# The first stage of a two-layer diffusion trunk: TensorE and SyncE in the source's own order, modulation rows as one stream

## Chip, core and metric

The kernel runs on one core of one Trainium2 chip. The metric is the device time of one execution in microseconds (us). Four compute engines matter: TensorE (PE in the profile, with PEld for its weight loads), VectorE (DVE), ScalarE (ACT), and SyncE (SP), whose queue issues nearly all loads from HBM.

## What is computed

A trunk of two layers over 256 latent tokens of width 2048, with 256 context tokens for the first layer. Cut to what matters here:

```python
s_lat, s_ctx = silu(c), silu(c_ctx)
for l in range(2):
    m = s_lat @ ada_w[l] + ada_b[l]                    # 2048 x 12288, six rows of modulation
    sh1, sc1, g1, sh2, sc2, g2 = split(m, 6)
    h = rms(xs, norm1_g[l]) * (1 + sc1) + sh1
    if l == 0:
        mc = s_ctx @ ada_w[l] + ada_b[l]
        hc = rms(ctx, norm1_g[l]) * (1 + csc1) + csh1
        y = attention(h, hc)                           # q, k, v by one input projection
    else:
        y = hyena(h)                                   # long convolution with filters from a small net
    xs = xs + g1 * y
    xs = xs + g2 * conv_ffn(rms(xs, norm2_g[l]) * (1 + sc2) + sh2)
```

The filters of the second layer (`_hyena_filters`: a net of three layers with sines, a projection to 2 x 2 x 2048 channels, a decay, a spectrum) depend on parameters alone. They, like the modulation rows, can be computed at any time before their use.

## The kernel before

Matrix products take the weights in chunks of 256 rows by 512 columns (`wload`, L321 to L324, 512 KB, from SyncE's queue). `wsplit` parts a chunk into a high and a low half (ACT cast L329, DVE subtraction L330), and `products` (L333 to L339) adds three products of halves. The tiles of `raw` have six buffers, `whi` and `wlo` three each, `araw` six. PSUM has eight banks; a `Ring` hands them out in turn.

The **first stage** ends when the first of the five key and value projections (`kv0`) is multiplied. Three pieces of work run in it beside each other:

- *Modulation rows for the first norm.* Scale (`j = 1`) and shift (`j = 0`) of 2048 columns each, latent and context together, in four groups `g` of 512 columns. `ada_block(g)` loads eight chunks for each `j`, two at a time, and multiplies them (L917: four matmuls of 32 rows by 512 columns for a pair of chunks, all into one bank `pv`). A block of eight chunks ends with a copy `st` by ACT (L921), a selection on PE (L924) into a bank `pt`, and DVE additions that write `adaV` and `cada` (L926) and the gains (L929). There are eight blocks, called ada10, ada00, ada11 and so on, each of four steps.
- *The filters.* `filter_net` (three layers, L539 to L549, each a matmul, a chain of DVE operations and a sine) and then `filters`: for each of four column groups and two orders a pair of filters. Each of the two has two `samples` (three matmuls L342 to L344 into a bank, DVE product with the decay L584, ACT cast L353, DVE rest L354, ACT absolute value L586, DVE maximum L589 from the second on). After the second of a pair `pn` sums the magnitudes on PE (L596 on DVE, then L599), and its reciprocal is taken by DVE (L571). `spectra` of a filter (two banks, six matmuls, one ACT copy L610, two DVE combinations L613, two stores) follow the samples of the next one. These generators are stepped by `bg`, with a credit of `START_RATE` per step of the modulation rows.
- *The norms* of the latent and the context rows. `stream_norm` loads the rows (L644), squares them (ACT L655, DVE additions L659), sums them over channels on PE and takes the inverse root on DVE (`rstd_of`, L371 to L387: L377 on PE, `newton`, L385 on DVE, L386 on PE), and multiplies (L664). `Normed.get` (L397 on) applies gain and shift and parts the result into halves (L415 to L420).

From the second group on, two chunks of `kv0` (`in_proj`, L744 on, 24 matmuls each) are put in per group; the last two follow behind the groups.

The instructions are traced in the order of the source, but the order on each engine's queue is set by a scheduler. It goes through all traced instructions with its own estimate of the times and picks the ready ones by priority. Each engine then works its queue strictly in that order. `tc.high_priority` raises the priority of a block of instructions: the weight matmuls of `ada_block` are in one.

The remaining ten modulation rows are computed from transposed weights by DVE, as weighted sums: `Ada.one` (L467 to L487) loads 512 KB on SyncE and, four steps later, multiplies and adds up a tile with one DVE instruction (L481). `drive` (L311) runs a stage and steps these sums at a rate per stage; `need` forces what is still missing when a row must be complete. `HY_ADA` is the rate of the second layer's input projection and `HO_ADA` that of its output projection. A list cell `calm[0]` puts the rate to zero while true; `proj_out` sets it anew for each of its groups (true in the last), and `ffn` for each of its eighths (true in the first two of the first chunk). The input projection of the second layer does not set it.

Of the kernel before, what the change touches and what calls it, by code (L numbers as in the profile page):

```python
# [21 lines left out]
T = 256  # L22
# [157 lines left out]
PI_F = 3.1415925  # L180


START_RATE = 2.0, 1.4
Q_RATE = 6.5
O_RATE = 5.2
KV_ADA, Q_ADA, O_ADA, HY_ADA, HO_ADA = 1.9, 0.7, 0.8, 0.2, 0.2
F0_ADA, F1_ADA = (0.7, 0.6), (0.4, 0.2)
EV_RATE, FLY, LAG = 1.0, 8, 4
F_RATE, HY_RATE, HO_RATE = 0.3, 1.2, 2.0
# [3 lines left out]
def trunk_kernel(ctx, tc, out, xT, cT, cols, rows, f_w0, f_w12, f_w3, ada_w, ada_t, w_in, w_out, hw_in, hw_out,  # L193
                 wg, wv, wd, k_tab, k_fg, k_z, k_decay):
    nc = tc.nc
# [172 lines left out]
        V.tensor_scalar(t, t, 0.375, 1.875, op0=ALU.mult, op1=ALU.add)  # L368
        V.tensor_tensor(y, y, t, op=ALU.mult)

    def rstd_of(accs, ps):  # L371

        pss = ps()
        n = len(accs)
        for tt in range(2):
            for i, a in enumerate(accs):
                PE.matmul(pss[:, tt: tt + 1], a[:, tt * P:(tt + 1) * P], ones[:, 0:1], start=i == 0, stop=i == n - 1)  # L377
        v = tiny([P, 2])
        V.tensor_scalar(v, pss[:, 0:2], 1.0 / D, EPS, op0=ALU.mult, op1=ALU.add)
        y = tiny([P, 2])  # L380
        newton(y, v, 2)
        pb = ps()
        dg = s2([P, T])
        for tt in range(2):
            V.tensor_scalar(dg[:, tt * P:(tt + 1) * P], ident, y[:, tt: tt + 1], None, op0=ALU.mult)  # L385
            PE.matmul(pb[:, tt * P:(tt + 1) * P], ones, dg[:, tt * P:(tt + 1) * P], start=True, stop=True)  # L386
        return pb[:, 0:T]  # L387

    def square_into(acc, x, first):
        if first:  # L390
# [249 lines left out]
    def load_x(src, name):  # L640
        g = []
        for i in range(4):
            t = q4([P, 4, T], F32, name)
            SP.dma_start(t, src[:, 4 * i:4 * i + 4])  # L644
            g.append(t)
        return g

    def stream_norm(src, res):
        xg = load_x(src, "x0")
        res.extend(xg)  # L650
        yield
        acc = None
        for g in range(4):
            sq = q4([P, 4, T], F32, "sq0")
            A.activation(sq, xg[g], AF.Square)  # L655
            if acc is None:
                acc = sq
            else:
                V.tensor_tensor(acc, acc, sq, op=ALU.add)  # L659
            yield  # L660
        pb = rstd_of([acc[:, k] for k in range(4)], ST)
        for g in range(4):
            for k in range(4):
                V.tensor_tensor(xg[g][:, k], xg[g][:, k], pb, op=ALU.mult)  # L664
            yield
# [236 lines left out]
    ftag[0] = Ring(6, 7, 2, 3)  # L902
    g0, gc0 = (pool.tile([P, KT], F32, tag="gain", bufs=2, name=nm("g")) for _ in range(2))

    def ada_block(g):

        gs = slice(4 * g, 4 * g + 4)

        tags = ("raw", "whi", "raw", "wlo"), ("raw", "araw", "raw", "araw")
        for j in (1, 0):  # L910
            lab[0] = f"ada{j}{g}"
            pv = AD()
            for i in range(0, 8, 2):
                raws = [wload(ada_w[i + n, 4 * j + g], tags[g > 0][(i + n) % 4]) for n in range(2)]
                with tc.high_priority():
                    for q in range(4):
                        PE.matmul(pv[32 * q:32 * q + 32], sl[:, 2 * i + q], raws[q // 2][:, q % 2],  # L917
                                  start=i == 0, stop=i == 6, tile_position=(0, 32 * q))
                yield
            st = s2([P, 512], F32, "adast")  # L920
            A.copy(st, pv)  # L921
            pt = AD()
            for b in range(4):
                PE.matmul(pt[:, 2 * b:2 * b + 2], st[:, b * P:(b + 1) * P], sel, start=True, stop=True)  # L924
            for s, dst in enumerate((adaV[:, 0, j, gs], cada[:, j, gs])):
                V.tensor_tensor(dst, pt[:, 0:8].rearrange("p (b s) -> p b s", s=2)[:, :, s], col("ada_b", j * KT + 4 * g, 4), op=ALU.add)  # L926
            if j == 1:
                for a, sc in ((g0, adaV[:, 0, 1, gs]), (gc0, cada[:, 1, gs])):
                    V.scalar_tensor_tensor(out=a[:, gs], in0=sc, scalar=1.0, in1=col("n1", 4 * g, 4), op0=ALU.add, op1=ALU.mult)  # L929

    bg.add(filter_net(), "filters")
    bg.add(filters(range(4)), "filters")
    norm_bg = Bg()
    xg, cg = [], []
    norm_bg.add(stream_norm(xT, xg), "nx")
    norm_bg.add(stream_norm(cT, cg), "nc")
    hN = Normed(xg, None, g0, adaV[:, 0, 0])
    cN = Normed(cg, None, gc0, cada[:, 0])
    KV0 = QC
    kvs = (("kv", KV0 + 2048, 0), ("k", KV0, 0), ("k", KV0 + 512, 1), ("v", KV0 + 1024, 0), ("v", KV0 + 1536, 1))  # L940
    for _ in range(3):
        bg.one()
    norm_bg.one()
    for _ in range(3):
        bg.one()
    first = None
    for g in range(4):
        for i, _ in enumerate(ada_block(g)):
            bg.step(START_RATE[g > 0])
            norm_bg.step(5.0)  # L950
            if g and i in (4, 7):
                lab[0] = "kv0"
                next(first)
        if not g:
            norm_bg.drain()
            ftag[0] = Ring(6, 7)
            banks = LO4.four()
            first = in_proj(kvs[0][1], banks, True)
        hN.get(g)
        cN.get(g)  # L960
    lab[0] = "kv0"
    for _ in range(3):
        bg.step(1.0)
    for _ in first:
        bg.step(4.0)
    bg.drain()
    spread_s(HI4)
    ada_bg.add(*ADA_LATER)
    attn_tables()
# [146 lines left out]
    accs = []  # L1116
# [195 lines left out]
```

## Time and profile before

| | |
|---|---|
| median of 3 runs | 2642.45 us (2640.13 to 2645.43) |
| profiled execution | 2640.06 us, span 2638.3 us |
| mean granted clock of TensorE | 0.976 |
| PE busy | 2525.4 us, 96% of the span |
| DVE busy | 1968.6 us, 75% |
| ACT busy | 1259.7 us, 48% |
| first stage, 0 to 246.2 us | PE busy 180.4 us |

A row of a timeline gives start, us, engine, source line, operation, the tile written and the tiles read (buffer numbers left out), shapes and count; in brackets the idle time of the engine just before it and what ended that. In a row of a group of instructions, the figures after the bar are busy us and the mean ns of one, then idle time before them with its releasers. A waits row gives the total, the number of waits and the longest. The granted clock is 1.00 at full speed.

### The profile page before, as it was taken

How to read it: one execution, taken by the hardware profiler on the slowest of the kernel's cores; microseconds unless marked ns; L12 is line 12 of the kernel's file. 1: busy time of each engine (PE TensorE's matmuls, PEld its weight loads, DVE VectorE, ACT ScalarE, POOL GpSimd, SP SyncE). 2: the span in 40 equal slices, each digit the busy share in tenths (PEclk: the TensorE clock that was granted, in tenths of full speed). 3: DMA queues.
4: the chain of work that ended last, by engine and by line, in shares of the span. 5: the costliest groups of instructions: out<-in, count | busy, mean ns of one | idle time of the engine just before them, and what ended most of it. 6: DMA issues, size and time to landing. Idle time of an engine off the chain costs nothing.

```text
span 2638.3 us, 48119 instructions
## 1 busy us (share of the span) xinstructions
PE 2525.4 (96%) x19502; PEld 2349.1 (89%) x19502; DVE 1968.6 (75%) x3073; ACT 1259.7 (48%) x1803; POOL 0.7 (0%) x6
## 2 busy tenths in 40 slices
PE   4788999999899999999999999999799999999999
PEld 2456888668899999999999999998799999999999
DVE  5656876987788888888886778889776755556664
ACT  3345223665354444445553656554354444445543
POOL 0000000000000000000000000000000000000000
PEclk7888999999999999999999999999899999999999
DMA  8685877655779999998898565555778766666664
GB/s 291 209 300 203 271 266 260 197 165 160 255 262 327 328 333 326 327 329 316 307 323 290 189 199 176 178 167 201 247 246 268 259 193 193 193 195 193 196 207 138
DMA packets 178870, 638.67 MB, mean 242 GB/s; under 512 B 20087, under 2 KB 20184, under 8 KB 178648
## 3 DMA queue, kind: packets, MB, share of 16 engines
q1 hardware_dynamic: 174040, 627.22, 71.5%
q10 hardware_dynamic: 4608, 8.39, 0.8%
q8 instruction: 152, 2.49, 0.4%
q14 instruction: 70, 0.57, 0.1%
HBM read 622.94 MB, written 12.58 MB: 241 GB/s over the span
## 4 chain that ended last, share of the span: by engine, by line
PE 89%; DVE 5%; ACT 3%; DMA 2%; issue 1%; SPq 0%; ACTq 0%; DVEq 0%
PE ps_proj L338 23%; PE ps_hy L338 9%; PE ps_kv L338 7%; PE ps_q L338 3%; PE ps_attn L846 1%; PE ps_ada L917 1%; PE ps_attn L807 1%; PE ps_ada L338 1%; DMA w<-f_w 1%; DVE araw_ada L481 1%; PE ps_conv L342 1%; DMA raw_kv<-w_in 1%; PE ps_filters L342 1%; PE ps_conv L343 1%; PE ps_conv L344 0%
## 5 line engine op out<-in xcount | busy, mean ns | idle before, releaser
L330 DVE TENSOR_TENSOR wlo_proj<-raw_proj,whi_proj 128x1024 fp32r<-128x1024 f32 x240 | 292.4, 1222 | 149.0 <-ACT whi_proj L329 147.1
L329 ACT CAST whi_proj<-raw_proj 128x1024 fp32r<-128x1024 f32 x240 | 252.0, 1054 | 306.9 <-PE ps_proj L338 271.6
L481 DVE SCALAR_TENSOR_TENSOR araw_ada<-araw_ada,slB 128x1024 f32<-128x1024 f32 x320 | 387.6, 1217 | 0.0
L338 PE MATMUL ps_proj<-ph,whi_proj 128*128 128x256 f32 x1408 | 192.4, 277 | 0.1
L338 PE MATMUL ps_proj<-ph,wlo_proj 128*128 128x256 f32 x1408 | 191.6, 276 | 0.0
L338 PE MATMUL ps_proj<-pl,whi_proj 128*128 128x256 f32 x1408 | 191.2, 276 | 0.0
L338 PEld LDWEIGHTS ps_proj<-ph,whi_proj 128*128 128x128 f32 x1408 | 174.3, 188 | 0.9 <-ACT whi_proj L329 0.9
L338 PEld LDWEIGHTS ps_proj<-ph,wlo_proj 128*128 128x128 f32 x1408 | 174.1, 188 | 0.2 <-DVE wlo_proj L330 0.2
L338 PEld LDWEIGHTS ps_proj<-pl,whi_proj 128*128 128x128 f32 x1408 | 174.1, 188 | 0.0
L329 ACT CAST whi_hy<-raw_hy 128x1024 fp32r<-128x1024 f32 x96 | 101.3, 1056 | 105.0 <-PE ps_hy L338 76.3
L330 DVE TENSOR_TENSOR wlo_hy<-raw_hy,whi_hy 128x1024 fp32r<-128x1024 f32 x96 | 116.3, 1221 | 44.2 <-ACT whi_hy L329 44.2
L338 PE MATMUL ps_hy<-hhi,whi_hy 128*128 128x256 f32 x768 | 109.1, 282 | 1.1 <-ACT hhi L418 1.1
L338 PE MATMUL ps_hy<-hlo,whi_hy 128*128 128x256 f32 x768 | 106.5, 280 | 0.0
L338 PE MATMUL ps_hy<-hhi,wlo_hy 128*128 128x256 f32 x768 | 104.3, 278 | 0.0
L338 PEld LDWEIGHTS ps_hy<-hhi,whi_hy 128*128 128x128 f32 x768 | 99.4, 190 | 3.4 <-ACT hhi L418 1.4
L338 PEld LDWEIGHTS ps_hy<-hlo,whi_hy 128*128 128x128 f32 x768 | 97.6, 190 | 0.8
L338 PEld LDWEIGHTS ps_hy<-hhi,wlo_hy 128*128 128x128 f32 x768 | 95.7, 188 | 0.1
L329 ACT CAST whi_kv<-raw_kv 128x1024 fp32r<-128x1024 f32 x40 | 42.0, 1053 | 110.7 <-PE ps_kv L338 82.5
L330 DVE TENSOR_TENSOR wlo_kv<-raw_kv,whi_kv 128x1024 fp32r<-128x1024 f32 x40 | 48.9, 1223 | 38.7 <-ACT whi_kv L329 38.7
L338 PE MATMUL ps_kv<-whi_kv,hhi 128*128 128x512 f32 x256 | 66.5, 400 | 0.0
L338 PE MATMUL ps_kv<-wlo_kv,hhi 128*128 128x512 f32 x256 | 64.0, 391 | 0.0
L338 PE MATMUL ps_kv<-whi_kv,hlo 128*128 128x512 f32 x256 | 63.9, 392 | 0.0
(9814 smaller groups left out, 7616.3 us busy)
## 6 DMA issues: line engine op xcount, KB each, us to landing
araw_ada<-ada_t SPq DMA_DIRECT2D x320, 512.0 KB, 5.1
raw_proj<-wd SPq DMA_DIRECT2D x176, 512.0 KB, 4.4
raw_hy<-hw_in SPq DMA_DIRECT2D x96, 512.0 KB, 3.8
raw_ada<-ada_w SPq DMA_DIRECT2D x46, 512.0 KB, 8.2
raw_kv<-w_in SPq DMA_DIRECT2D x40, 512.0 KB, 4.9
raw_q<-w_in SPq DMA_DIRECT2D x32, 512.0 KB, 4.6
raw_proj<-w_out SPq DMA_DIRECT2D x32, 512.0 KB, 4.5
raw_proj<-hw_out SPq DMA_DIRECT2D x32, 512.0 KB, 4.5
```

The costliest lines, as they stand in the source:

```text
L329: A.copy(hi, raw)
L330: V.tensor_tensor(lo, raw, hi, op=ALU.subtract)
L338: PE.matmul(o, ll if p == 2 else lh, rl if p == 1 else rh, start=first and p == 0, stop=last and p == 2, skip_group_check=True)
L342: PE.matmul(o, lh, rh, start=first, stop=False, **kw)
L343: PE.matmul(o, lh, rl, start=False, stop=False, **kw)
L481: V.scalar_tensor_tensor(out=raw, in0=raw, scalar=1.0, in1=slB[:, h * 1024:(h + 1) * 1024], op0=ALU.mult, op1=ALU.mult, accum_out=acc[:, h ...
L807: PE.matmul(ss_[m], qT[64 * m:64 * m + 64, h % 4, q_], KTa[h // 2][64 * m:64 * m + 64, h % 2], start=True, stop=True)
L846: PE.matmul(o[:, 0:P], wT[:, kt * P:(kt + 1) * P], v, start=kt == 0, stop=kt == 3)
L917: PE.matmul(pv[32 * q:32 * q + 32], sl[:, 2 * i + q], raws[q // 2][:, q % 2], start=i == 0, stop=i == 6, tile_position=(0, 32 * q))
```

## The change

Inside the first stage, TensorE and SyncE no longer take their order from the scheduler: `tc.manual_schedule` keeps their instructions in the order of the source. The other engines are still scheduled. The modulation rows become one generator, `ada_stream`. Where a block ended with copy, selection and additions at once, `columns` now does the copy at the block's end and the selection one step later, behind the first weight matmuls of the next block; its bank comes from the filters' ring instead of the blocks' own. Both norms' rows are loaded before the stream starts. The inverse root (`rstd_steps`) becomes two steps, with three steps of the norm's queue between. The rates change: 1.5 filter steps per step of the rows in the first group and 1.8 in the others (2.0 and 1.4 before), 3 norm steps instead of 5, and two steps of the filters ahead of the stream instead of six. `HY_ADA` goes from 0.2 to 0.3 and `HO_ADA` from 0.2 to 0.4.

```diff
-START_RATE = 2.0, 1.4
+START_RATE = 1.5, 1.8
...
-KV_ADA, Q_ADA, O_ADA, HY_ADA, HO_ADA = 1.9, 0.7, 0.8, 0.2, 0.2
+KV_ADA, Q_ADA, O_ADA, HY_ADA, HO_ADA = 1.9, 0.7, 0.8, 0.3, 0.4
...
-    def rstd_of(accs, ps):
+    def rstd_steps(accs, ps):
...
         newton(y, v, 2)
+        yield
         pb = ps()
...
-        return pb[:, 0:T]
+        yield pb[:, 0:T]
...
-    def stream_norm(src, res):
-        xg = load_x(src, "x0")
-        res.extend(xg)
-        yield
+    def stream_norm(xg):
...
-        pb = rstd_of([acc[:, k] for k in range(4)], ST)
+        rest = rstd_steps([acc[:, k] for k in range(4)], ST)
+        next(rest)
+        for _ in range(3):
+            yield
+        pb = next(rest)
...
+    def ada_stream():
+        def columns(g, j, pv):
+            gs = slice(4 * g, 4 * g + 4)
             st = s2([P, 512], F32, "adast")
             A.copy(st, pv)
-            pt = AD()
+            yield
+            pt = ftag[0]()
...
+            else:
+                hN.get(g)
+                cN.get(g)
+            yield
+
+        before = None
+        for g in range(4):
+            tags = ("raw", "araw", "raw", "araw") if g else ("raw", "whi", "raw", "wlo")
+            for j in (1, 0):
+                pv = AD()
+                for i in range(0, 8, 2):
+                    raws = [wload(ada_w[i + n, 4 * j + g], tags[(i + n) % 4]) for n in range(2)]
+                    for q in range(4):
+                        PE.matmul(pv[32 * q:32 * q + 32], sl[:, 2 * i + q], raws[q // 2][:, q % 2],
+                                  start=i == 0, stop=i == 6, tile_position=(0, 32 * q))
+                    if before:
+                        next(before)
+                        before = None
+                    yield g, 4 * (j == 0) + i // 2
+                before = columns(g, j, pv)
+                next(before)
+        next(before)
...
-    for _ in range(3):
-        bg.one()
-    norm_bg.one()
-    for _ in range(3):
-        bg.one()
-    first = None
-    for g in range(4):
-        for i, _ in enumerate(ada_block(g)):
+    with tc.manual_schedule(engines={nc.tensor.engine, nc.sync.engine}):
+        for _ in range(2):
+            bg.one()
+        xg.extend(load_x(xT, "x0"))
+        cg.extend(load_x(cT, "x0"))
+        norm_bg.add(stream_norm(xg), "nx")
+        norm_bg.add(stream_norm(cg), "nc")
+        first = None
+        for g, i in ada_stream():
             bg.step(START_RATE[g > 0])
-            norm_bg.step(5.0)
+            norm_bg.step(3.0)
             if g and i in (4, 7):
                 lab[0] = "kv0"
                 next(first)
```

Line numbers move with the edits: L599 of before is L603 after, L917 is L942, L924 is L921, L386 is L387, L481 is L485.

How the rows stand on SyncE's queue near the program's start, first before the change. `raw_ada` are chunks of weights for the modulation rows, `x` the latent (`xT`) or context (`cT`) rows:

```order
L323 DMA raw_ada_153_564<-ada_w 128x1024
L323 DMA raw_ada_174_640<-ada_w 128x1024
L644 DMA x_308<-cT 128x1024
L644 DMA x_310<-cT 128x1024
L644 DMA x_312<-cT 128x1024
L644 DMA x_314<-cT 128x1024
L323 DMA raw_ada_175_642<-ada_w 128x1024
```

The same place after it:

```order
L648 DMA x_144<-xT 128x1024
L648 DMA x_146<-cT 128x1024
L648 DMA x_148<-cT 128x1024
L648 DMA x_150<-cT 128x1024
L648 DMA x_152<-cT 128x1024
L323 DMA raw_ada_46_155<-ada_w 128x1024
L323 DMA raw_ada_47_157<-ada_w 128x1024
```

The four loads of context rows stood behind fourteen loads of weights; now they stand ahead of the first.

On PE, in the first group, before (`ps_nc` is the context rows' norm, `ps_ada` a block of the modulation rows):

```order
L377 MATMUL ps_nc_375<-ones_67,sq_364 128x1 x8
L386 MATMUL ps_nc_398<-s_399,ones_67 128x128 x2
L342 MATMUL ps_filters_485<-w_349,fah_176 128x512
L343 MATMUL ps_filters_485<-w_349,fah_176 128x512
L344 MATMUL ps_filters_485<-w_349,fal_177 128x512
L917 MATMUL ps_ada_124_464<-raw_ada_125_465,sl 32x512 x2
L917 MATMUL ps_ada_124_464<-raw_ada_126_467,sl 32x512 x2
L917 MATMUL ps_ada_124_464<-raw_ada_133_495,sl 32x512 x2
L917 MATMUL ps_ada_124_464<-raw_ada_134_497,sl 32x512 x2
L917 MATMUL ps_ada_124_464<-raw_ada_144_533,sl 32x512 x2
```

And after it, the second block of the rows, between its second and its third pair of chunks:

```order
L942 MATMUL ps_ada_88_314<-raw_ada_100_354,sl 32x512 x2
L342 MATMUL ps_filters_360<-w_259,fah_211 128x512
L343 MATMUL ps_filters_360<-w_259,fah_211 128x512
L344 MATMUL ps_filters_360<-w_259,fal_212 128x512
L603 MATMUL ps_filters_371<-ones_67,hf_290 128x1 x4
L342 MATMUL ps_filters_376<-fhl_284,fm_249 128x512
L343 MATMUL ps_filters_376<-fhl_285,fm_249 128x512
L344 MATMUL ps_filters_376<-fhl_284,fm_249 128x512
L342 MATMUL ps_filters_377<-fhl_284,fm_249 128x512
L343 MATMUL ps_filters_377<-fhl_285,fm_249 128x512
L344 MATMUL ps_filters_377<-fhl_284,fm_249 128x512
L377 MATMUL ps_nc_395<-ones_67,sq_344 128x1 x8
```

A block's sixteen matmuls stood together, behind the context norm; now pairs of chunks stand between filter matmuls, and `pn` (L603) stands right behind the sample matmuls from which its magnitudes come.

On DVE, ahead of the last mixer, before (`t` are the steps of the inverse root, `araw_ada` the weighted sums of modulation rows):

```order
L379 TENSOR_SCALAR t_20631<-ps_proj_3349_20620 128x2
L481 SCALAR_TENSOR_TENSOR araw_ada_20113,asum_14253<-araw_ada_20113,slB_86 128x1024
L359 TENSOR_SCALAR t_20634<-t_20631 128x2
L481 SCALAR_TENSOR_TENSOR araw_ada_20274,asum_14253<-araw_ada_20274,slB_86 128x1024
L360 TENSOR_SCALAR t_20633<-t_20634 128x2
L481 SCALAR_TENSOR_TENSOR araw_ada_20583,asum_14253<-araw_ada_20583,slB_86 128x1024
L362 TENSOR_TENSOR t_20634<-t_20633 128x2
L481 SCALAR_TENSOR_TENSOR araw_ada_20586,asum_14253<-araw_ada_20586,slB_86 128x1024
L363 SCALAR_TENSOR_TENSOR t_20634<-t_20634,t_20631 128x2
L481 SCALAR_TENSOR_TENSOR araw_ada_20589,asum_14253<-araw_ada_20589,slB_86 128x1024
```

And after it:

```order
L379 TENSOR_SCALAR t_20634<-ps_proj_3349_20623 128x2
L485 SCALAR_TENSOR_TENSOR araw_ada_20338,asum_14256<-araw_ada_20338,slB_86 128x1024
L359 TENSOR_SCALAR t_20637<-t_20634 128x2
L485 SCALAR_TENSOR_TENSOR araw_ada_20417,asum_14256<-araw_ada_20417,slB_86 128x1024
L360 TENSOR_SCALAR t_20636<-t_20637 128x2
L485 SCALAR_TENSOR_TENSOR araw_ada_20604,asum_14256<-araw_ada_20604,slB_86 128x1024
L362 TENSOR_TENSOR t_20637<-t_20636 128x2
L330 TENSOR_TENSOR wlo_ffn1.0_3367_20710<-raw_ffn1.0_3365_20707,whi_ffn1.0_3366_20709 128x1024
L363 SCALAR_TENSOR_TENSOR t_20637<-t_20637,t_20634 128x2
```

Before, nine weighted sums stand between the steps of the inverse root there; after, three, and six more stand earlier, in the output projection of the second layer.

More of the change, by code (lines that the diff above doesn't have):

```diff
@@ L386, in rstd_of @@
             PE.matmul(pb[:, tt * P:(tt + 1) * P], ones, dg[:, tt * P:(tt + 1) * P], start=True, stop=True)
-        return pb[:, 0:T]
+        yield pb[:, 0:T]
+    def rstd_of(accs, ps):
+        return list(rstd_steps(accs, ps))[1]
     def square_into(acc, x, first):
@@ L903, in trunk_kernel @@
     g0, gc0 = (pool.tile([P, KT], F32, tag="gain", bufs=2, name=nm("g")) for _ in range(2))
[L905 to L919, printed above, removed]
+    def ada_stream():
+        def columns(g, j, pv):
+            gs = slice(4 * g, 4 * g + 4)
             st = s2([P, 512], F32, "adast")
             A.copy(st, pv)
-            pt = AD()
+            yield
+            pt = ftag[0]()
             for b in range(4):
@@ L929, in ada_block @@
                     V.scalar_tensor_tensor(out=a[:, gs], in0=sc, scalar=1.0, in1=col("n1", 4 * g, 4), op0=ALU.add, op1=ALU.mult)
+            else:
[8 more added lines that the diff above has]
+                for i in range(0, 8, 2):
+                    lab[0] = f"ada{j}{g}"
+                    raws = [wload(ada_w[i + n, 4 * j + g], tags[(i + n) % 4]) for n in range(2)]
[9 more added lines that the diff above has]
+        next(before)
     bg.add(filter_net(), "filters")
@@ L934, in trunk_kernel @@
     xg, cg = [], []
-    norm_bg.add(stream_norm(xT, xg), "nx")
-    norm_bg.add(stream_norm(cT, cg), "nc")
     hN = Normed(xg, None, g0, adaV[:, 0, 0])
@@ L953, in trunk_kernel @@
                 next(first)
[L954 to L966, printed above, removed]
+            if (g, i) == (0, 7):
+                norm_bg.drain()
+                ftag[0] = Ring(6, 7)
+                banks = LO4.four()
+                first = in_proj(kvs[0][1], banks, True)
+        lab[0] = "kv0"
+        for _ in first:
+            bg.step(4.0)
+        bg.drain()
     spread_s(HI4)
```

## The prediction

> **What bounds the kernel now.** I read the busy time by stage first. Columns: stretch, length, busy us (and instructions) of PE, PE's weight loads, DVE, ACT, POOL, then PE's granted clock, the DMA share and GB/s.
>
> ```profile
> 0.00:77.70 77.70, 42.12 (x154) 22.39 (x154) 46.53 (x121) 22.92 (x35) 0.70 (x6) 0.74 0.71 257
> 77.70:206.50 128.80, 105.55 (x536) 64.36 (x532) 79.00 (x153) 62.27 (x114) 0.00 (x0) 0.89 0.77 269
> 206.50:246.20 39.70, 32.71 (x133) 25.30 (x130) 23.86 (x60) 19.62 (x43) 0.00 (x0) 0.83 0.61 217
> 246.20:300.00 53.80, 53.80 (x232) 42.39 (x231) 38.54 (x74) 19.55 (x36) 0.00 (x0) 1.00 0.68 227
> ```
>
> From 246.2 us on PE has no idle time, so whatever the first stage gains or loses there is passed on one to one. In the first 246.2 us PE is busy for 180.4, at a clock below full. No other engine is full either: DVE 149.4, ACT 104.8, DMA share about 0.7. So the stage is set by the order in which work stands on each queue. PE's timeline shows where (start, us, operation, idle before it and who ended it); the cuts of the table above are the ends of the second and the eighth block of modulation rows (L917) and of kv0's last product.
>
> ```profile
> 9.00 1.11 PE L539 MATMUL ps_filters<-s,s 64*64 64x256 f32 x2 [3.39 <-ACT s L549]
> 12.82 3.14 PE L917 MATMUL ps_ada<-raw_ada,sl 128*32 128x512 f32 x8 [2.71 <-DVE s L546]
> 29.62 1.05 PE L917 MATMUL ps_ada<-raw_ada,sl 128*32 128x512 f32 x4
> 52.02 1.86 PE L599 MATMUL ps_filters<-ones,hf 128*128 128x1 f32 x8 [5.16 <-DVE hf L596]
> 54.32 0.63 PE L343 MATMUL ps_filters<-fhl,fm 128*128 128x512 f32 x1
> 54.75 0.63 PE L344 MATMUL ps_filters<-fhl,fm 128*128 128x512 f32 x1
> 58.21 0.39 PE L343 MATMUL ps_filters<-w,fah 128*128 128x512 f32 x1
> 58.44 0.40 PE L344 MATMUL ps_filters<-w,fal 128*128 128x512 f32 x1
> 64.86 3.57 PE L377 MATMUL ps_nc<-ones,sq 128*128 128x1 f32 x16 [6.03 <-DVE sq L659]
> 73.42 4.37 PE L917 MATMUL ps_ada<-raw_ada,sl 128*32 128x512 f32 x32
> 97.02 3.64 PE L917 MATMUL ps_ada<-raw_ada,sl 128*32 128x512 f32 x32 [3.16 <-ACT adast L921]
> 203.79 2.76 PE L917 MATMUL ps_ada<-raw_kv,sl 128*32 128x512 f32 x24
> 244.41 2.00 PE L338 MATMUL ps_ada<-whi_kv,hlo 128*128 128x512 f32 x8
> ```
>
> Between 30.7 and 73.4 us no row of weights is multiplied; then a whole block comes in one lump of 4.4 us. A matmul of 512 columns starts every 0.43 us at 54 us (half clock) and every 0.23 us at 58 us. SyncE's queue, and its longest wait in the first 250 us, show the same hole from the side of the loads:
>
> ```profile
> 28.03 4.17 SPq L644 DMA_DIRECT2D x<-cT  x4
> 41.08 5.22 SPq L323 DMA_DIRECT2D raw_ada<-ada_w  x4
> 55.06 0.33 SPq L323 DMA_DIRECT2D raw_kv<-ada_w  x1
> SPq L323 <- PE ps_ada L917: 58.5, 19, 17.4
> ```
>
> The context rows `cT` are asked for behind fourteen weight loads; PE's matmuls of its norm stand ahead of the second block and wait 6.03 us for its squares; the block holds the buffers; SyncE waits 17.4 us at a stretch for one.
>
> **The change, part by part.** *Start.* Four loads of 512 KB (`cT`) now precede the first weights. The rate by 6.25 us slices:
>
> ```profile
> GB/s 176 402 406 337 409 409 400 341 115 75 0 42 252 334 86 110 329 344 271 141 273 365 245 370 327 213 144 345 351 212 343 348 194 326 369 369 81 79 161 95
> ```
>
> At about 405 GB/s each takes 1.3 us, so the first weight matmul goes from 12.8 to about 18.0 us, a loss of 5.2 at most, since PE waits there for a filter layer too. It buys the end of the hole: all later weights find free buffers as long as PE consumes them two by two.
>
> *First two blocks.* Before, they end at 77.7 us with 42.1 busy. After: 18.0, plus 39.9 of work (42.1 less 2.2 for two layers of the filter net, done by then), less 6.5 for 15 filter matmuls that the new order has later (21 against 36, at 0.43), plus waits. The waits on PE's side, before:
>
> ```profile
> PE ps_filters L342 <- ACT w L353: 11.2, 4, 4.8
> PE ps_filters L599 <- DVE hf L596: 10.7, 3, 5.2
> PE ps_ada L917 <- ACT adast L921: 5.7, 2, 3.2
> PE ps_nx L386 <- DVE s L385: 2.6, 1, 2.6
> ```
>
> I keep 3.5 for L599, 2.6 for the first norm's second half (the second's is covered by the weight and filter matmuls put between) and 4, an estimate between 0 and 7, for the filter net's layers, which now stand behind weight matmuls. 18.0 + 33.4 + 10 = 61.4, say 62.
>
> *The six blocks that follow.* Work: 105.6 x 0.89 = 94 us at full clock. The new order has 159 filter matmuls here against 123 and 120 of kv0 against 128: 28 more at 0.23 is 6.4, and one more L599 and L924 group about 2. So 102, and at the same clock 102 / 0.89 = 115. Waits: what goes are the late loads of filter weights (11.2 us in four waits; they are now asked for many blocks ahead) and the block's bank (`adast`, 5.7), as its copy and its selection are now two steps apart. What comes is the price of source order: `pn` (L603, before L599) stands right behind the sample matmuls that feed it, in six of eight places without a kv0 product between. Its chain, from the groups of the first 251 us:
>
> ```profile
> L584 DVE TENSOR_TENSOR hf<-ps_filters,dec 128x512 f32<-128x512 f32 x32 | 21.4, 686 | 15.4 <-PE ps_filters L344 15.4
> L613 DVE SCALAR_TENSOR_TENSOR spo<-ps_filters,se 128x512 f32<-128x512 f32 x32 | 21.0, 685 | 10.7 <-PE ps_filters L344 6.3 <-issue 1.5 <-ACT hhi L416 1.2
> L589 DVE TENSOR_TENSOR hf<-hf,hf 128x512 f32<-128x512 f32 x16 | 10.8, 689 | 1.3 <-ACT hf L586 1.0
> L596 DVE TENSOR_TENSOR hf<-hf,hf 128x512 f32<-128x512 f32 x8 | 5.5, 689 | 0.2
> L353 ACT CAST fhl<-hf 128x512 fp32r<-128x512 f32 x32 | 19.4, 619 | 46.0 <-DVE hf L584 45.6 <-DVE hlo L420 0.3
> L586 ACT ACTIVATE hf<-hf 128x512 f32<-128x512 f32 x32 | 19.4, 625 | 4.5 <-DVE fhl L354 4.3
> ```
>
> 0.69 + 0.62 + 0.63 + 0.69 + 0.69 is 3.3 us, with its hand-overs 3.5. Four of the six fall in this stretch: 14 us. Two banks serve samples, spectra, `pn` and now also the modulation's selection; a bank read by two L613 (1.3 us) holds the sample behind it, about 1 us for each of six pairs: 6. Sum 20, against 23 before (128.8 less 105.6). The bounds are 6, if weight and kv0 matmuls cover most of them, and 53, if none (below). 115 + 20 = 135.
>
> *The end of the stage.* 32.7 x 0.83 = 27 at full clock, less 13 matmuls (3.0) and about 1 of the sums that spread the conditioning row, which come later: 23, or 26 at 0.89; one L603 wait with what is left of the last norm's tail is 4. So 30, and kv0 ends at 62 + 135 + 30 = 227 instead of 246.2: 19 gained. The added steps of the norms and of the stream add no instruction of weight (cost 0; the same matmuls and squares are issued), and from kv1 to the middle of the second layer all engines keep their order.
>
> *Late rates.* `HY_ADA` is read only where `calm[0]` is false; the first mixer leaves it true and the next `proj_out` is the first to clear it, so 0.2 to 0.3 moves nothing. `HO_ADA` counts: 28 of 32 steps advance it, 5 units before (28 x 0.2), 11 after, and the forced rest ahead of the last mixer falls from 11 to 5. There DVE is what PE waits for (first and last weighted sum of the nine between the norm's steps, then PE's next matmul, and a stretch of the convolutions before it):
>
> ```profile
> 1893.98 0.16 DVE L379 TENSOR_SCALAR t<-ps_proj 128x2 f32<-128x2 f32 x1 [1.81 <-PE ps_proj L377]
> 1894.06 1.22 DVE L481 SCALAR_TENSOR_TENSOR araw_ada<-araw_ada,slB 128x1024 f32<-128x1024 f32 x1
> 1895.27 1.22 DVE L481 SCALAR_TENSOR_TENSOR araw_ada<-araw_ada,slB 128x1024 f32<-128x1024 f32 x1
> ...
> 1903.79 1.22 DVE L481 SCALAR_TENSOR_TENSOR araw_ada<-araw_ada,slB 128x1024 f32<-128x1024 f32 x1
> 1907.43 0.48 DVE L385 TENSOR_SCALAR s<-ident,t 128x128 f32<-128x128 f32 x2
> 1907.77 1.22 PE L386 MATMUL ps_proj<-s,ones 128*128 128x128 f32 x4 [13.82 <-DVE s L385]
> 1780.00:1840.00 60.00, 57.70 (x424) 52.29 (x424) 56.91 (x101) 27.35 (x40) 0.00 (x0) 1.00 0.57 198
> ```
>
> Nine sums become three: 6 x 1.215 = 7.3 us, less 0.7 for small steps that they hid. Three of the six land in the convolutions' end, where DVE has 3.1 us free in 60 and needs 3.6: a cost between 0 and 3.7, I take 2.6. Net 4.0.
>
> **Sum.** 19 + 4 = 23. The profiled execution took 2640.06 us (span 2638.3 and 1.8 around it), 2.4 under the median of the runs; from the median, 2642.45 - 23 = 2619.
>
> **The rivals.** *Waits covered* (chance 0.17): weight and kv0 matmuls cover the filters' chain and keep the clock up. For: six of the largest waits above are of things that came late, not of work. Against: PE's order is fixed, so a cover works only where it stands. Six blocks in 102 + 6, end in 26, start in 60: kv0 ends at 194, 52 gained, with the late part 56: 2586.
>
> *The clock* (0.18): PE slows after short waits. After the wait of 5.16 us the matmuls run at half speed for six us. At a granted 0.80 instead of 0.89 the six blocks take 102 / 0.80 + 20 = 148: 13 less gained, 2632. The Trainium skill, "TensorE: Matmul & The Clock Gate", Part 1 (the HAM clock gate), has PE fall to half rate once it idles for a window of about 3.4 us and come back after about as long of steady work. By that rule the 3.5 us at L603 would trip it each time; the trace agrees at 52 us.
>
> *Slower: two banks in line* (0.12). PE can no longer step over a filter matmul whose bank is not free. A pair of filters (its samples, spectra and one `pn`) is then one chain: two L613 1.3 us, sample 0.7, L584 0.7, half a spectrum 0.7, two L613 1.3, sample 0.7, the 3.5 above, L603 1.0, a spectrum 1.4: 11.3, with hand-overs 12. A pair's share of weight and kv0 matmuls (216 for seven pairs, 0.23 each, and a selection: 8 us, 9 at the clock of 0.89) comes on top, as does DVE's other work (79.0 us less 5.1 pairs of 16 operations of 0.69, over seven pairs: 3.3). 24 us for each of seven pairs is 168 instead of 135: kv0 ends at 260, 14 lost, 4 regained: 2652. It decides from 39 us of waits in the six blocks, 5.6 for a pair.
>
> *Only the late part works* (0.10): the six blocks take 154, where gain and loss of the first stage cancel: 2638.
>
> **How the numbers follow.** The forecast has 0.43. A measurement of this kernel can tell 0.2%, 5.3 us, from no change. Faster by more: forecast, covered and clock, 0.78; same: 0.10; slower: 0.12. The range runs from 2592, which leaves out most of the covered case, to 2642, which takes in the case without a gain and leaves out the slower one.
>
> **What would show it.** Right: the second block of weights ends near 62 us, weight matmuls in pairs at even distances, no stretch without DMA before 200 us, PE waiting about 3.5 us at L603 in six places, kv0's last product near 227, and three weighted sums instead of nine between L379 and L386 near the last mixer, PE's wait there 7 us. Wrong: PE's waits in the six blocks above 39 us or under 8, a granted clock under 0.80 there, the last mixer's wait unchanged, or a gap after kv0 that was not there.

## The result, and the profile after

The changed kernel is slower: 2674.7 us in the median of four runs (2668.7 to 2676.8), beside 2641.3 us for the kernel before in the same measurement. The ratio is 1.012, with an interval of 1.010 to 1.014. The profiled execution is the fastest of the four, 2668.7 us with a span of 2666.9, which is 28.6 us more than the 2638.3 of before; what the other runs take beyond it, the trace cannot tell.

The stage table of the kernel after has its cuts at the same events as the one in the prediction: the end of the second and of the eighth block of modulation rows, and kv0's last product.

```profile
0.00:70.70 70.70, 36.79 (x148) 17.82 (x149) 41.41 (x115) 21.50 (x32) 0.70 (x6) 0.76 0.73 264
70.70:243.20 172.50, 125.79 (x567) 74.67 (x566) 90.98 (x176) 67.07 (x122) 0.00 (x0) 0.82 0.62 215
243.20:278.30 35.10, 26.49 (x105) 20.42 (x106) 18.24 (x48) 21.66 (x49) 0.00 (x0) 0.85 0.59 211
```

The first two blocks did become shorter, 70.7 us instead of 77.7. The six blocks that follow take 172.5 us instead of 128.8. kv0's last product ends at 278.3 instead of 246.4, 31.9 us late (the 246.2 of the prediction is where the matmul behind it starts). The loss in the whole span is 28.6, so 3.3 us come back behind it. In the middle stretch PE is busy for 125.8 us at a clock of 0.82 and idle for 46.7; before it was busy for 105.6 at 0.89 and idle for 23.2.

Four rows of PE's waits up to the end of kv0 name the place (who waits, for whom, us in all, times, longest):

```profile
PE ps_filters L603 <- DVE hf L600: 42.6, 6, 9.4
PE ps_x L942 <- DMA raw_ada<-ada_w: 12.0, 1, 12.0
PE ps_filters L342 <- ACT w L353: 9.4, 4, 6.4
PE ps_nx L387 <- DVE s L386: 4.5, 1, 4.5
```

Nearly half of PE's 89.2 idle us are spent in front of the column sums `pn` (L599 before, L603 now), which cost 10.7 us before. PE's timeline shows seven of the eight places; the last one, at 249.20, waits 6.32 us:

```profile
55.67 1.87 PE L603 MATMUL ps_filters<-ones,hf 128*128 128x1 f32 x8 [8.23 <-DVE hf L600]
87.93 1.86 PE L603 MATMUL ps_filters<-ones,hf 128*128 128x1 f32 x8 [9.04 <-DVE hf L600]
113.86 1.05 PE L603 MATMUL ps_filters<-ones,hf 128*128 128x1 f32 x8
143.65 1.84 PE L603 MATMUL ps_filters<-ones,hf 128*128 128x1 f32 x8 [9.42 <-DVE hf L600]
145.92 0.63 PE L343 MATMUL ps_filters<-fhl,fm 128*128 128x512 f32 x1
146.35 0.63 PE L344 MATMUL ps_filters<-fhl,fm 128*128 128x512 f32 x1
167.74 1.84 PE L603 MATMUL ps_filters<-ones,hf 128*128 128x1 f32 x8 [5.33 <-DVE hf L600]
194.91 1.03 PE L603 MATMUL ps_filters<-ones,hf 128*128 128x1 f32 x8
219.15 1.86 PE L603 MATMUL ps_filters<-ones,hf 128*128 128x1 f32 x8 [4.27 <-DVE hf L600]
```

The six places that wait are the six that the prediction counted: those with no kv0 product between the sample and its sums. The two with such products wait for nothing. A wait costs twice: the sums behind it take 1.84 us and more instead of 1.05, and the next 512-column matmuls start every 0.43 us, the distance that the prediction read as half clock. VectorE's timeline tells why the wait of 9.42 us is not 3.5:

```profile
134.27 0.69 DVE L588 TENSOR_TENSOR hf<-ps_filters,dec 128x512 f32<-128x512 f32 x1 [0.57 <-PE ps_filters L344]
135.09 0.76 DVE L424 TENSOR_TENSOR hlo<-x,hhi 128x256 fp32r<-128x256 f32 x2
...
139.87 0.76 DVE L424 TENSOR_TENSOR hlo<-x,hhi 128x256 fp32r<-128x256 f32 x2 [0.83 <-ACT hhi L420]
140.69 0.69 DVE L354 TENSOR_TENSOR fhl<-hf,fhl 128x512 fp32r<-128x512 f32 x1
142.08 0.69 DVE L593 TENSOR_TENSOR hf<-hf,hf 128x512 f32<-128x512 f32 x1 [0.69 <-ACT hf L590]
142.81 0.69 DVE L600 TENSOR_TENSOR hf<-hf,hf 128x512 f32<-128x512 f32 x1
```

The sample is there at 134.3. Then VectorE runs the norm's halves of the group that the modulation rows have just made ready (`hN.get`, `cN.get`: eight L424 up to 140.6, paced by ScalarE's own copies of the same group), and only then the magnitudes' chain. Nothing on VectorE or ScalarE steps over that block, and nothing on PE steps over the column sums. The Trainium skill, "TensorE: Matmul & The Clock Gate" (Part 1, on the queues under "Architectural detail"), calls VectorE's and ScalarE's queues strictly first in, first out; these rows agree.

Behind kv0, the longest waits of the kernel after:

```profile
PE ps_proj L387 <- DVE s L386: 12.8, 3, 7.7
PE ps_proj L338 <- DVE wlo_proj L330: 6.8, 10, 1.1
```

and the same two of the kernel before:

```profile
PE ps_proj L386 <- DVE s L385: 18.9, 3, 13.8
PE ps_proj L338 <- DVE wlo_proj L330: 3.7, 6, 1.0
```

The norm ahead of the last mixer waits 6.1 us less, the projection into which the moved sums went 3.1 more. That is a net gain of 3.0, close to the 3.3 above.

### The profile page after: what moved, and what is told of

Its sections match the earlier page's. It is cut to its first block, busy times and chain, and to the rows that moved or that the text cites. A ratio compares the mean times of both kernels' runs of the same rounds, so it can differ in the third digit from the quotient of the medians.

```text
span 2666.9 us, 48113 instructions
## 1 busy us (share of the span) xinstructions
PE 2533.4 (95%) x19502; PEld 2350.3 (88%) x19502; DVE 1969.4 (74%) x3073; ACT 1260.1 (47%) x1803; POOL 0.7 (0%) x6
## 5 line engine op out<-in xcount | busy, mean ns | idle before, releaser
L485 DVE SCALAR_TENSOR_TENSOR araw_ada<-araw_ada,slB 128x1024 f32<-128x1024 f32 x320 | 387.6, 1217 | 0.0
```

The lines of the kernel that those rows point to most:

```text
L485: V.scalar_tensor_tensor(out=raw, in0=raw, scalar=1.0, in1=slB[:, h * 1024:(h + 1) * 1024], op0=ALU.mult, op1=ALU.mult, accum_out=acc[:, h ...
```

## The experiments

Two theories went in. *W*: PE's fixed order makes it stand in front of the column sums, and what it waits for is VectorE's and ScalarE's queue. *S*: SyncE's fixed order brings the rows late. Line numbers shift by a few in the edited kernels; where the column sums became a function they are L585.

### The late rates alone

```diff
-KV_ADA, Q_ADA, O_ADA, HY_ADA, HO_ADA = 1.9, 0.7, 0.8, 0.2, 0.2
+KV_ADA, Q_ADA, O_ADA, HY_ADA, HO_ADA = 1.9, 0.7, 0.8, 0.3, 0.4
```

(on the kernel before)

> The kernel before with the two late rates alone (HY_ADA 0.3, HO_ADA 0.4). If the prediction's term (d) holds, it is 3 to 5 us faster than before (ratio 0.998 to 0.999), with all of it at the sums that stand behind the last mixer. Rival: the sums that move displace work elsewhere and nothing is left (ratio 1.000, within 0.0005). The after trace shows about 32 us lost up to the end of kv0 and 28.6 us lost in all, which leaves 3 to 4 us of gain behind it.

Ratio 0.9988 (0.9975 to 1.0001): 3.2 us by the middle of it, in the expected size, while the interval just reaches no change (the medians differ by 1.0 us). Its trace has the same two waits as after, 12.8 us and 6.8 us. Its first stage has no edit, and kv0 ends at 243.9, so two executions of that stage differ by 2.5 us.

By its waits the late part of the change is worth about 3 us; the runs alone do not tell that from nothing. The whole loss lies in the first stage.

### The manual order taken away, whole and by halves

```diff
-    with tc.manual_schedule(engines={nc.tensor.engine, nc.sync.engine}):
+    with nullcontext():
```

> The kernel after without the manual order, so that the scheduler orders TensorE and SyncE as before, with the stream, the stepped norms, the rates and everything else kept. Theory W: the column sums stand further back again and the loss goes: 2630 to 2650 us. If instead the stream and the norms' steps themselves cost the time, it stays at 2660 us or more. Rival S gives 2635 to 2650 us too, and is told apart by the two kernels with the column sums moved.

Ratio 0.997 (0.996 to 0.999): faster than before by 7 us, and than after by 39. Its kv0 ends at 244.3 us, and PE's waits at the column sums up to there are 5.1 us:

```profile
PE ps_filters L603 <- DVE hf L600: 5.1, 2, 4.1
```

The stream, the norms' steps and the rates cost nothing. What they gain is open: about 3 of the 7 us are the late rates', and 244.3 lies between the ends of kv0 in the two executions of the unchanged first stage (246.4 and 243.9). The scheduler puts the column sums somewhere else, as at 80.61 us, between products of kv0:

```profile
79.69 1.08 PE L338 MATMUL ps_ada<-wlo_kv,hhi 128*128 128x512 f32 x4
80.61 0.95 PE L603 MATMUL ps_filters<-ones,hf 128*128 128x1 f32 x8
81.43 0.72 PE L338 MATMUL ps_ada<-wlo_kv,hhi 128*128 128x512 f32 x2
```

The halves: `engines={nc.tensor.engine}` and `engines={nc.sync.engine}`.

> The kernel after with only TensorE in the source's order; SyncE's issues are left to the scheduler. Theory W: TensorE's order is the loss, 2662 to 2678 us, six waits at the column sums of 35 us or more. Rival S (SyncE's order of the transfers is the loss): 2635 to 2650 us.

> The kernel after with only SyncE in the source's order; TensorE is left to the scheduler. Theory W: near the kernel without manual order, 2632 to 2645 us. Rival S: 2660 us or more.

With TensorE alone in the source's order: 1.017 (1.014 to 1.019), 2685.9 us, 8 us above the expected range, kv0 ending at 291.8; the six waits at L603 are 42.6 us again, as in after. With SyncE alone: 1.0043 (1.003 to 1.006), 2654.6 us, 10 us above what theory W expected. So TensorE's order is the larger part, about 50 us against the scheduled kernel; SyncE's order costs 19 us where TensorE is free, and gives 11 back where TensorE is not. The two do not add.

### The column sums moved

Behind the spectra's six products of the same step (`pn_behind`), then further, behind the first products of the next filter sample (`pn_step`):

```diff
-            pn = ftag[0]()
-            for c in range(4):
-                PE.matmul(pn[:, c:c + 1], mags[0][:, c * P:(c + 1) * P], ones[:, 0:1], start=True, stop=True)
+            due.append((mags[0], invn[:, o, dc * 4:dc * 4 + 4]))
             mags.clear()
-            late.append((invn[:, o, dc * 4:dc * 4 + 4], pn[:, 0:4]))
...
                 split(hl[0][:, tt], hl[1][:, tt], h)
+                if not i and not tt:
+                    sums()
```

(`sums()` emits the four matmuls for what is in `due`. In `pn_behind` it is called behind the spectra instead.)

> The kernel after, with the four column sums of the magnitudes and their bank moved behind the six spectra products of the same step. Theory W (TensorE's head-of-line wait at the column sums is the loss): the six products cover about 2.7 us of each of the six waits (42.6 us in all), less 1 us each for the bank that the spectra now take from the last sample: 8 to 18 us faster than after, 2657 to 2667 us. Rival D (VectorE and ScalarE have no time to spare there, and the same work is awaited at the next product): no faster than 2670 us. Rival S (the weights' transfers in the source's order set the pace): the same as after.

> The kernel after, with the column sums moved further, behind the first products of the next filter sample, so that six spectra products and mostly eight weights products (7 us and more) stand in front of them. Theory W: less than 8 us are left of the 42.6 us of waits, 6 to 10 us come up at the banks, the half clock behind the waits goes (8 us): 25 to 40 us faster than after, 2635 to 2650 us. Rival D: the wait comes back at the samples that follow, 2665 us or more. Rival S: as after, 2670 to 2677 us.

`pn_behind`: 1.007 (1.005 to 1.010), 2662.0 us, 13 us faster than after. That is in the expected range, but not for the expected reason:

```profile
PE ps_filters L585 <- DVE hf L609: 37.5, 6, 8.3
PE ps_filters L585 <- ACT se L620: 5.8, 1, 5.8
```

PE still waits 43.3 us at the column sums (42.6 in after). What went is the wait for the split of the filter weights, 9.4 to 0.5 us on ScalarE and 3.2 to 0.7 on VectorE; probably the split is now done while PE stands at the sums. So this run agrees with theory W in its number only.

`pn_step`: 1.0054 (1.003 to 1.008), 2658.5 us: 16 us faster than after, less than the 25 expected of W, more than rival D's 10. PE's waits tell where the rest went:

```profile
PE ps_filters L342 <- ACT w L353: 23.2, 4, 7.7
PE ps_nc L377 <- DVE sq L669: 7.3, 1, 7.3
PE ps_filters L585 <- DVE hf L611: 5.9, 1, 5.9
```

36.7 us of waits at the column sums are gone, and 13.8 have come up at the next thing that ScalarE feeds, the split of the filter weights (9.4 to 23.2), 7.3 more at the context norm's squares. ScalarE's timeline at one of those waits (7.26 us, ended at 194.15):

```profile
186.23 1.09 ACT L419 ACTIVATE x<-x,adaV,g 128x256 f32<-128x256 f32 x2
...
190.41 0.69 ACT L420 CAST hhi<-x 128x256 fp32r<-128x256 f32 x2
191.01 0.58 ACT L622 ACTIVATE se<-ps_filters 128x512 f32<-128x512 f32 x1
192.35 1.03 ACTq L627 DMA_DIRECT2D spec<-spo  x2
193.48 0.62 ACT L353 CAST w<-w 128x512 fp32r<-128x512 f32 x1 [1.88 <-DVE spo L625]
```

The same block of norm halves stands ahead again, this time of another customer.

### The norm halves in pieces

```diff
-            else:
-                hN.get(g)
-                cN.get(g)
             yield
...
+            if g and i < 4:
+                lab[0] = "kv0"
+                hN.get(g - 1, [i])
+                cN.get(g - 1, [i])
```

(`get` takes a list of pieces; one of four is done in each of four weights steps.)

> The kernel after, with each group's norm halves (two tiles of four pieces, 6 to 6.5 us in one run on VectorE and ScalarE) made one piece a weights step over four steps, the column sums where after has them. Theory W2 (what the column sums wait for is the block of halves that VectorE and ScalarE were given ahead of the magnitudes): the waits of 9.04 and 9.42 us fall to the bare chain of 4 to 4.5 us, the wait of 6.37 us for the weights' split falls to 1, the others stay: 10 to 20 us faster than after, 2655 to 2665 us. Rival C (the chain itself is 8 to 9 us): no faster than 2668 us.

> Both edits: column sums behind the next sample's first products, and norm halves in pieces. Theory W2: what was left with the column sums moved, three waits of 6.7 to 7.7 us for ScalarE's split of the filter weights (23.2 us in all with a small one), stood behind the block of halves and falls to 1 us each: 15 to 25 us faster than with the column sums moved alone, 2634 to 2644 us. Rival F (the filter weights' load comes late from SyncE's queue): the waits stay, 2652 us or more.

`get_split`, where the column sums stand as in after: 1.006 (1.004 to 1.008), 2659.7 us, 15 faster than after. The two waits with the block ahead of them fell, from 9.04 and 9.42 us, the second nearly to the 4.27 us of the chain without the block:

```profile
86.51 1.87 PE L603 MATMUL ps_filters<-ones,hf 128*128 128x1 f32 x8 [5.89 <-DVE hf L600]
137.62 1.84 PE L603 MATMUL ps_filters<-ones,hf 128*128 128x1 f32 x8 [4.58 <-DVE hf L600]
```

The others stayed (8.24, 5.32, 4.27, 6.32). Rival C, a chain that is 8 to 9 us by itself, is out. Both edits together: 1.0036 (1.002 to 1.005), 2651.4 us, 7 faster than `pn_step` where 15 or more were expected. 16.9 us of waits for the split of the filter weights remain.

### The small loads off SyncE's queue

```diff
-            SP.dma_start(dec, k_decay[:, :, dc * 512:(dc + 1) * 512])
+            G.dma_start(dec, k_decay[:, :, dc * 512:(dc + 1) * 512])
...
-                    SP.dma_start(raw[d * HW:(d + 1) * HW], w3v[:, o, d, dc * 512:(dc + 1) * 512])
+                    G.dma_start(raw[d * HW:(d + 1) * HW], w3v[:, o, d, dc * 512:(dc + 1) * 512])
```

> The kernel after, with the loads of the filter weights and of the decay issued on GpSimd's queue instead of SyncE's. Theory S2 (a second head-of-line wait, on SyncE: a small load that waits for its buffer holds back the modulation rows behind it, 32 us at the filter weights and 7 us at the decay in after): the transfers' hole between 50 and 100 us closes and the time falls by 6 to 19 us, 2655 to 2668 us (19 us is what SyncE's order alone cost over the scheduler's). Rival (TensorE's waits at the column sums set the pace and the rows would only arrive earlier): 2668 to 2677 us.

> TensorE and SyncE in the source's order with all three repairs: column sums further back, norm halves in pieces, and the two small loads on GpSimd's queue. If the three waits are all that the manual order lost, it comes to 2630 to 2643 us, level with the kernel before or better. If the halves' pieces that VectorE and ScalarE still hold ahead of the filters' work remain (three waits of 3.4 to 6.1 us for the weights' split and one of 5.9 us at the column sums), it stays at 2645 to 2652 us.

> Only SyncE in the source's order, TensorE left to the scheduler, and the two small loads issued on GpSimd. If those loads are SyncE's head-of-line wait (12 to 15 us each in the longest cases), the rows come on time again: 10 to 19 us faster than 2655 us, 2636 to 2645 us. If it is the order of the rows themselves: 2650 us or more.

On the kernel after it is no gain: 1.015 (1.013 to 1.017), 7 us slower than after, with intervals that overlap. SyncE's longest waits in it, from 30 to 250 us, are put down to the weights matmuls themselves (102.1 us in 16 waits):

```profile
SPq L323 <- PE ps_ada L942: 102.1, 16, 19.4
```

By this row, the modulation rows wait for buffers that PE, standing at its column sums, has not read. Only the semaphore that comes last is named, so it shows more surely that they still wait than for whom: in after the same line has 115.4 us in 15 waits, under `spec<-spo`. With TensorE in the source's order, theory S is out. With all three repairs (`repaired`) it is 1.0047 (1.003 to 1.006), no better than with two. With TensorE free (`sp_pool`), the same edit brings 2654.6 us down to 2640.8, 0.9996 (0.9985 to 1.0007): 14 us, as expected. SyncE's timeline without it (`sp_only`):

```profile
40.32 12.63 SPq L323 DMA_DIRECT2D raw_ada<-ada_w  x6
53.05 0.58 SPq L625 DMA_DIRECT2D dec<-k_decay  x1
68.94 1.12 SPq L629 DMA_DIRECT2D w<-f_w  x2
```

and with it (`sp_pool`), where GpSimd issues the same filter weights at 67.15:

```profile
40.15 13.62 SPq L323 DMA_DIRECT2D raw_ada<-ada_w  x7
53.86 0.48 SPq L323 DMA_DIRECT2D raw_kv<-w_in  x1
54.43 14.49 SPq L323 DMA_DIRECT2D raw_ada<-ada_w  x6
```

The two loads of 128 KB for the filter weights, for which no buffer is free yet, hold every row behind them for 15 us; from 50 to 75 us the DMA share is 0.40 in the first and 0.93 in the second. So SyncE has a head-of-line wait of its own, which shows only where TensorE has none.

### The filter weights split earlier

Loads of the next filter weights moved ahead of the second pair of samples, their split ahead of the spectra, on top of `get_split_pn`:

```diff
                 for i in range(2):
+                    if i and after:
+                        coming = load(*after, dec)
                     hl = [q4([P, 2, 512], F32R, "fhl") for _ in range(2)]
                     yield from samples(o, dc, i, w3, dec, hl)
+                    if i and after:
+                        dec, w3 = parts(*coming)
```

> Column sums further back and norm halves in pieces, as before, and now the filter weights (and decay) loaded two samples ahead and split one spectra step ahead of their first use, with TensorE and SyncE still in the source's order. If the 17 us of waits for that split are what is left of the loss, they fall below 5 us: 8 to 18 us faster than 2651 us, 2633 to 2643 us. If the wait only moves to the next product that VectorE or ScalarE feeds, 2646 us or more.

1.0019 (1.001 to 1.003), 2646.3 us: 5 us gained of the 8 to 18 expected, kv0 ending at 254.1. The waits for that split are gone, and others stand in their place:

```profile
PE ps_ada L338 <- ACT whi_kv L329: 11.2, 3, 4.6
PE ps_nc L377 <- DVE sq L681: 9.0, 1, 9.0
PE ps_filters L585 <- DVE hf L611: 7.3, 3, 4.3
```

kv0's own weights, which waited 0.8 us in after, now wait 11.2. PE is still idle for 68.8 us, against 53.6 in the scheduled kernel.

### The scheduled kernel, further

The stream without manual order, with the small loads on GpSimd, with the norm halves in pieces, and with both:

> The kernel without manual order, with the two small loads on GpSimd's queue. The scheduler puts those loads where their buffers are nearly free (17 us of waits at them are left of SyncE's): 0 to 8 us faster than without that, 2627 to 2636 us. Rival: no change, since after 185 us the stage waits for the filters and not for rows (DMA share 0.25 there), 2633 to 2638 us.

> The same with the norm halves in pieces. If the block of halves costs under the scheduler's order too (two waits for the weights' split of 6.8 us and below), 3 to 8 us faster than the one before, 2622 to 2632 us; if the scheduler had already put the block where nobody waits, no change.

> No manual order, norm halves in pieces, small loads on SyncE. If the pieces are what made the last of the scheduled kernels faster, 2626 to 2634 us and level with it or better; if it was the queue together with the pieces, 2634 to 2640 us.

The small loads alone: 1.0005 (0.999 to 1.002), 8.8 us slower than `sched`, though kv0 ends at 244.3 and 244.4 in the profiled executions; that difference stays unexplained. Both: 0.996 (0.9945 to 0.997). The pieces alone: 0.995 (0.993 to 0.997), 2629.0 us, the fastest kernel of the study and faster than both given ones; kv0 ends at 232.1 instead of 244.3, though its interval still touches that of `sched` (0.996 to 0.999) and overlaps that of both edits together.

The first stage of the kernels, from their profiled executions (us; idle and busy are PE's up to the end of kv0):

```text
kernel            kv0 ends   idle   busy   ratio to before
before             246.4     65.8  180.6   1
after              278.3     89.2  189.1   1.0121
pe_only            291.8     95.9  196.0   1.0167
pool_loads         288.0     92.0  196.0   1.0149
pn_behind          270.8     77.9  193.0   1.0072
get_split          269.7     79.7  190.0   1.0059
pn_step            264.7     72.9  191.8   1.0054
repaired           264.5     69.3  195.2   1.0047
get_split_pn       259.8     66.9  192.9   1.0036
early_w            254.1     68.8  185.3   1.0019
sp_only            257.3     56.8  200.5   1.0043
sp_pool            245.3     52.8  192.5   0.9996
sched              244.3     53.6  190.7   0.9973
sched_split        232.1     46.2  185.9   0.9949
```

By these ends of kv0 the gains over after are smaller than by the medians of the runs: 7.5 us for `pn_behind` (13 by the medians), 13.6 for `pn_step` (16), 8.6 for `get_split` (15), 18.5 for `get_split_pn` (23), 24.2 for `early_w` (28) and 34.0 for `sched` (39). The profiled execution of after is 6 us under its median, which is about the difference.

## Why the prediction was wrong, point by point

*The bound.* Right: what the first stage loses, 31.9 us, is passed on one to one; only the late part's gain stands between it and the span's 28.6.

*First two blocks: 62 predicted, 70.7 measured.* The first weight matmul came at 17.7 us (18.0 predicted). The column sums there waited 8.23 us instead of 3.5, which is 4.7 of the 8.7 missed; the norm's second half waited 4.5 instead of 2.6, and PE was busy for 35.7 us behind 17.6 instead of 33.4. (By SyncE's timeline seventeen loads of weights stood ahead of the context rows, not fourteen; the sum does not use that number.)

*The six blocks: 135 predicted, 172.5 measured. This is the step that failed.* The work was right: 125.8 us at 0.82 are 103 us at full clock, 102 predicted. PE was busy for 125.8 us instead of 115, 10.8 more, nearly all of it the clock of 0.82 instead of 0.89. The waits were 46.7 us instead of 20, which is 26.7: 14.1 at the column sums, 9.4 for the split of the filter weights and 3.1 for the blocks' copy `adast`, both of which the prediction put at nothing. "0.69 + 0.62 + 0.63 + 0.69 + 0.69 is 3.3 us, with its hand-overs 3.5" priced the chain as if VectorE and ScalarE were idle when it starts. The chain took 4.27 us where only steps of the sample before it stood between (219.15), a small error; where the norm halves or squares stood ahead it took 8 to 9.4, and 5.33 with one split of kv0's weights between (167.74). The four waits of this stretch make 28.1 us (9.04, 9.42, 5.33, 4.27) instead of 14. `get_split` shows the mechanism: with the block in pieces, the 9.42 became 4.58 and the 9.04 became 5.89. The prediction fixed PE's order and left the other two engines' order out of the price, although the scheduler still sets it and the stream issues the norm halves right after the selection, ahead of the filter step.

*"What goes are the late loads of filter weights (11.2 us ... they are now asked for many blocks ahead)".* Wrong: only 5.1 of the 11.2 us lay in the six blocks before, and 9.4 us of waits for their split lie there in after. The longest, 6.37 us at 204.81, stands behind the same block in ScalarE's queue; the other three, 3.0 us together, have no block ahead.

*The end: 30 predicted, 35.1 measured.* The column sums there wait 6.32 us, with splits of kv0's weights ahead on VectorE, and kv0 waits 2.5 us for the last norm halves, where 4 was allowed for wait and tail.

*Late part: 4.0 predicted, 3.0 measured* by the two rows of waits. The terms were 7.3 less 0.7 less 2.6; the longest wait fell from 13.8 to 7.7 us, 6.1, and the projection took 3.1 back.

*The rivals.* "Two banks in line" gave 2652 for a slower kernel and named 39 us of waits in the six blocks as the point from which it decides; 46.7 came. But its mechanism is not what happened: PE's waits for a bank (L342 for `spo`, `se`, `hf` and `cada`) are 3.8 us up to the end of kv0. "The clock" is half right: at 0.82 it took about 10 us, behind waits that were longer than foreseen. "Waits covered" is out by the same row of 42.6 us.

*Of the cause, what is shown and what is not.* Shown: the manual order of the two queues costs 39 us, TensorE's being the larger part (`sched`, `pe_only`, `sp_only`); the column sums' place and the norm halves' block each cost about 15 of it (`pn_step`, `get_split`; 14 and 9 by the end of kv0), and together 23 (18.5). With these and the earlier split, 28 of the 39 are recovered (24 of 34 by the end of kv0). What remains, about 11 us, is spread over waits of another kind at each repair (`early_w`); no single one was found to carry it. VectorE and ScalarE in the source's order too was not tried.

## What to carry to other kernels

Fixing the order of one engine turns every late operand into a wait of everything behind it. So price such a wait with what the *feeding* engines have queued ahead of the chain, read from their own order, and not with the chain's length. A repair of one such wait often moves it to the next consumer of the same queue: 36.7 us removed at one place brought 16 us of time. Before fixing an order by hand, time the same restructured code under the scheduler: here that was 0.997 (0.995 with the halves in pieces), and the fixed order was the whole loss.

## What the runs showed of the hardware that was not expected

*Half clock early in a wait.* In the kernel before, PE idles 2.80 us ahead of the column sums at 87.27; the wait begins at 84.47, when the clock is still full:

```profile
82.24 0.50 PE L343 MATMUL ps_filters<-fhl,fm 128*128 128x512 f32 x1 [0.97 <-DVE fhl L354]
83.53 0.47 PE L342 MATMUL ps_filters<-fhl,fm 128*128 128x512 f32 x1 [0.56 <-ACT hf L586]
87.27 1.87 PE L599 MATMUL ps_filters<-ones,hf 128*128 128x1 f32 x8 [2.80 <-DVE hf L596]
```

The table by stretches (the clock is the third number from the right) reads 1.00 up to 85.2 us and 0.50 behind it, 0.7 us into that wait:

```profile
81.80:85.20 3.40, 1.67 (x5) 0.78 (x5) 2.79 (x5) 2.12 (x3) 0.00 (x0) 1.00 1.04 369
85.20:85.40 0.20, 0.00 (x0) 0.00 (x0) 0.02 (x1) 0.15 (x1) 0.00 (x0) 0.50 0.98 215
```

The Trainium skill, "TensorE: Matmul & The Clock Gate" (Part 1, the HAM clock gate), lets the clock fall after an idle window of about 3.4 us. Here no idle time was that long: in the 3.4 us before the fall PE was busy for 1.67 us, with no gap longer than 0.97. The wait of 2.75 us at 176.75 is nearer to the page: there the clock falls at 177.3, 3.3 us behind the last filter matmul and within the first column sums. All six waits of after, 4.27 us and longer, are followed by half clock, as the page has it.

*A slower stretch that the clock column does not show.* In the profiled executions of four kernels (`sched_split_pool`, `get_split_pn`, `sp_only`, `repaired`) PE does 172 matmuls per 20 us in most of 200 us of a part where it has no idle time, and 178 or 179 in the others, at a reported clock of 1.00 in both. From 740 to 980 us the scheduled kernel does 2120 matmuls, `sched_split_pool` 2066:

```profile
740.00:980.00 240.00, 240.00 (x2120) 240.00 (x2119) 202.35 (x286) 114.90 (x140) 0.00 (x0) 1.00 0.92 328
```

```profile
740.00:980.00 240.00, 240.00 (x2066) 240.00 (x2066) 196.12 (x275) 109.76 (x131) 0.00 (x0) 1.00 0.90 318
```

54 matmuls of 0.113 us are 6 us; runs of one kernel differ by up to 15 us here (2637 to 2652 us for the kernel before in one measurement). Its cause was not looked for. It can hide a gain of the first stage in a single execution: `sched_split_pool` ends kv0 10 us before `sched` and has the same span, and this stretch is 6 of the 10.
